# Applying the S5 norm factor at PSUM eviction of the output projection's first half instead of on its input

## The chip, the cores and the metric

The kernel runs on one core of a Trainium2 chip. Its engines work side by side, each from its own queue in program order: TensorE (PE, matmuls; PEld is its weight load), VectorE (DVE), ScalarE (ACT), GpSimd (POOL) and SyncE (SP, which only issues transfers here). The metric is the device time of one execution in microseconds.

## What is computed

One layer of a decoder for 320 token columns (256 of a prompt and 64 of eight short samples): a gated delta-rule group of eight heads and an S5 group, whose outputs are joined into one output projection, then a SwiGLU feed-forward block. What matters here, cut from the reference:

```
y5 = jax.nn.gelu(y5.reshape(bsz, t, MIX_B)).astype(x.dtype)
ab = y5 @ w_glu
y5 = ab[..., :MIX_B] * jax.nn.sigmoid(ab[..., MIX_B:])
y5 = rmsnorm(y5, g_s5_out)

mix = jnp.concatenate([o, y5], axis=-1) @ w_out
```

`rmsnorm` divides each token by the root of its mean square and multiplies by a gain per channel (`g_s5_out`). Tokens are columns here, so the norm is one factor per column, the same for all channels, and the gain is one per row.

## The kernel before

Activations are stored transposed: 128 channels by 320 tokens a tile, 16 tiles for the model's 2,048 channels. To reach nearly full fp32 accuracy with the faster fp32r matmul, both operands are split into a high and a low part (hi, lo), and `mm3` issues three matmuls for each 128x128 weight tile: hi by hi, hi by lo, lo by hi. Such a trio is called a group below; the trace shows it as two `ps_mm<-hT,whi` and one `ps_mm<-hT,wlo`. Weights arrive by DMA as `raw` tiles (512 KB, from SP's queue, line 472), ScalarE makes `whi` (line 501) and VectorE `wlo` (line 502); twelve weight buffers are shared by raw, hi and lo.

The order on every engine is fixed when the program is built. The main sequence is a list of weight segments (`Seg`), and after each group `tick` lets background generators (`bg`) add instructions whose inputs a planner's clock believes ready. An engine then works through its queue in that order and stands where an instruction's inputs are late. Several background generators run in the stretch of this change: the eight heads of the delta rule (`delta`, with `sample` for the sample columns), which use the PSUM tiles `ps_bA` and `ps_bB`; and the modulation (`ada`, `ps_ax`), whose segments are mixed into the list.

The stretch goes so. The GLU of the S5 group (`body_g`, `body_a`) makes eight tiles y5(m), kept in `u`, and squares of them are summed in `sqa` (the last one in `sql`, which has the name `gt` in the trace). Then `y5_norm` multiplies both by a matrix of ones to get the sum over channels in every row, takes Ln and Exp for the factor r, and for each of the eight tiles multiplies by r in place, takes a slot of the tag `h`, and writes hi and lo with the gain into a tile `hT`. The output projection's first half (`first_pair` for output tiles 0 and 1, `first_half` for tiles 2 to 15) contracts these eight tiles: 16 output tiles by 8 groups, 128 groups. `store` copies each result from PSUM (two banks of `ps_mm`) on ScalarE into `u` (tiles 0 to 7) or `M` (8 to 15). The second half contracts the eight heads' outputs (`hz` in the trace) and adds. The heads must all be done by its start.

SP's queue is in order too: a weight load placed behind a store of a head's result is issued only when that store's data exist.

Of the kernel before, what the change touches and what calls it, by code (L numbers as in the profile page):

```python
# [10 lines left out]
F32 = mybir.dt.float32  # L11
F32R = mybir.dt.float32r
AF = mybir.ActivationFunctionType
OP = mybir.AluOpType
# [9 lines left out]
N = NP + NS  # L24
# [86 lines left out]
class Layer:  # L111
# [2015 lines left out]
    def mixer(self):  # L2127
        I = self.I

        self.items += self.ada_set(self.ADA[0], self.ADA[1])  # L2130
        self.yps = {}
        self.y5 = lambda m: self.u[:, m].rearrange("p h w -> p (h w)")[:, :N]
        act_y = lambda kt: (self.yT[kt][:, 0], self.yT[kt][:, 1])
        glu, self.gt5 = [], {}
        for m in range(8):
            def body_g(s, m=m):
                self.await_(lambda: len(self.yT) == 8 and self.npg == 0)
                self.npg += 1
                ps = self.mbank()
                self.mm3(s, ps[:, :N], 0, act_y, True, True)  # L2140
                self.pend += 1
                self.bg(self.glu_gate(m, ps), front=True)

            def body_a(s, m=m):
                self.await_(lambda: self.nga == 0)
                self.nga += 1
                ps = self.mbank()
                self.mm3(s, ps[:, :N], 0, act_y, True, True)
                self.pend += 1
                self.bg(self.glu_tail(m, ps), front=True)  # L2150

            glu.append(Seg(I["w_glu"][0], 0, 8, 1024 + m * 128, 128, body_g))
            glu.append(Seg(I["w_glu"][0], 0, 8, m * 128, 128, body_a))
        self.items += merge(glu, self.ada_set(self.ADA[1], self.ADA[2]))
        self.fn(lambda: self.give("h", 8))
        self.fn(lambda: self.bg(self.y5_norm(), front=True))
        self.items += self.ada_set(self.ADA[2], self.ADA[3])
        wo = I["w_out"][0]
        self.M = [None] * 16
        act_m = lambda kt: (self.mT[kt][:, 0], self.mT[kt][:, 1])  # L2160

        def first_half(s, m):
            self.await_(lambda: all(k in self.mT for k in range(8, 16)))
            ps = self.mbank()
            self.mm3(s, ps[:, :N], 0, act_m, True, True)
            store(m, ps)

        def first_pair(s):
            self.await_(lambda: all(k in self.mT for k in range(s.k0, s.k0 + 4)))
            self.nomm = s.k0 == 8  # L2170
            if self.nomm:
                self.wps = self.mbank(), self.mbank()
            for m in range(2):
                self.mm3(s, self.wps[m][:, :N], m, act_m, s.k0 == 8, s.k0 == 12)
                if s.k0 == 12:
                    store(m, self.wps[m])

        def store(m, ps):
            if m < 8:
                self.M[m] = self.y5(m)  # L2180
            elif m % 2 == 0:
                self.await_(lambda: self.used["h"] < self.CAP["h"])
                self.used["h"] += 1
                t = self.htmp("M")
                self.M[m], self.M[m + 1] = t[:, 0:N], t[:, N:2 * N]
            self.copy(self.M[m], ps[:, :N])

        a = [Seg(wo, k0, 4, 0, 256, first_pair) for k0 in (8, 12)]
        a += [Seg(wo, 8, 8, m * 128, 128, lambda s, m=m: first_half(s, m)) for m in range(2, 16)]
        self.items += merge(a, self.ada_set(self.ADA[3], self.ADA[4]))  # L2190

        def heads():
            self.give("h", 8)

        self.fn(heads)

        def second_half(s, m):
            self.await_(lambda: all(k in self.mT for k in range(8)))
            if m == 0:
                self.post_start(0, 2, "g_post_mix")  # L2200
            ps = self.mbank()
            self.mm3(s, ps[:, :N], 0, act_m, True, True)
            self.pend += 1
            self.bg(self.post_chunk(m, ps, 2), front=True)

        self.items += [Seg(wo, 0, 8, m * 128, 128, lambda s, m=m: second_half(s, m)) for m in range(16)]
# [15 lines left out]
    def glu_tail(self, m, ps):  # L2222
        while m not in self.gt5:
            yield
        t = self.gt5.pop(m)
        y = self.y5(m)
        yield from self.p.stt(y, t[:, :N], 1.0, ps[:, :N], OP.add, OP.mult)
        self.nga -= 1
        self.pend -= 1
        yield  # L2230
        if m == 0:
            yield from self.take("xw")
        yield from self.acc_square(y, m == 0, t, m == 7)
        if m == 7:
            return
        self.give("xw")
# [20 lines left out]
    def y5_norm(self):  # L2257

        while self.nsq < 7:
            yield  # L2260
        r = self.sql
        yield from self.until("PE", (), (self.sqa[:, :N], self.sql[:, :N]))
        while self.bank_free("mm") > self.clk["now"]:
            yield
        ps = self.bank("mm")
        self.mm(ps[:, :N], self.onesc, self.sqa[:, :N], True, False)
        self.mm(ps[:, :N], self.onesc, self.sql[:, :N], False, True)
        self.act(r[:, :N], ps[:, :N], AF.Ln, scale=1.0 / 4096, bias=self.c_eps)
        self.exp(r[:, :N], r[:, :N], scale=-0.5, bias=self.c_lnh)
        yield  # L2270
        g = self.gcols("g_s5_out")
        for m in range(8):
            y = self.y5(m)
            yield from self.p.mul(y, y, r[:, :N])
            yield
            yield from self.take("h")
            hl = self._slot(self.hp.tile([128, 2, N], F32R, name="hT", tag="h", bufs=self.hbufs), "h", self.hbufs)
            yield from self.p.act(hl[:, 0], y, AF.Copy, scale=g[:, m:m + 1])
            yield
            yield from self.p.stt(hl[:, 1], y, g[:, m:m + 1], hl[:, 0].bitcast(F32), OP.mult, OP.subtract)  # L2280
            self.mT[8 + m] = hl
        self.give("xw", 2)


    def post_start(self, i, gate, g):
# [267 lines left out]
def merge(a, b):  # L2553

    out, i, j = [], 0, 0
    while i < len(a) or j < len(b):
        if j * len(a) < i * len(b) and j < len(b) or i >= len(a):
            while b[j].hold:
                out.append(b[j])
                j += 1  # L2560
            out.append(b[j])
            j += 1
        else:
            out.append(a[i])
            i += 1
    return out
# [37 lines left out]
```

## Time and profile before

| | us |
|---|---|
| three runs | 1861.14, 1871.71, 1873.30 (median 1871.71) |
| the profiled execution | 1872.74 |
| its span from first to last instruction | 1871.0 |
| TensorE busy | 1774.1 (95%) |
| VectorE busy | 961.3 (51%) |
| ScalarE busy | 763.8 (41%) |
| GpSimd busy | 316.8 (17%) |
| mean granted TensorE clock | 0.969 of full |

A row of a timeline gives start, length, engine, line, operation, output<-inputs, count, and in brackets how long the engine stood idle before and what released it. Matmul lengths overlap (a weight load and the next matmul begin before one ends), so distances between starts are used for TensorE's pace. [...]

### The profile page before, as it was taken

Reading aid. Unit: us, or ns where it says so; the run is one execution under the profiler, and the core shown is the slowest. Engines: PE = TensorE matmul, PEld = TensorE weight load, DVE = VectorE, ACT = ScalarE, POOL = GpSimd, SP = SyncE. Lnnn points to the kernel's source line nnn. Section 1 sums busy time; section 2 is a strip of 40 time slices with the busy share of each in tenths; the row PEclk is TensorE's granted clock in tenths of the full one; section 3 lists DMA queues with packets and bytes.
Section 4 is the critical chain, followed back from the end, with each engine's and each line's share of the span. In section 5 each row is a group of like instructions: output and inputs, shape, how many; then the busy total and the mean of one; then the engine's idle time right before and its main releaser. Section 6 shows DMA issues by size and latency. Waiting matters only on the chain.

```text
span 1871.0 us, 32687 instructions
## 1 busy us (share of the span) xinstructions
PE 1774.1 (95%) x12971; PEld 1609.3 (86%) x12971; DVE 961.3 (51%) x1798; ACT 763.8 (41%) x1438; POOL 316.8 (17%) x429
## 2 busy tenths in 40 slices
PE   7899998899999898998999999999999999999998
PEld 4778996666787676897799999999999999999997
DVE  3677733888756356444734334344443444444445
ACT  3433334575643255443534333333333333333343
POOL 1000184656031221026500000000000000000043
PEclk9999988999999897999999999999999999999999
DMA  8998644767848762867555566554565545655452
GB/s 277 304 357 282 173 103 141 207 188 212 265 139 268 227 185 84 261 191 236 171 169 169 155 185 178 150 153 120 153 176 150 147 121 153 177 148 153 124 144 86
DMA packets 501262, 340.66 MB, mean 182 GB/s; under 512 B 45355, under 2 KB 452619, under 8 KB 500781
## 3 DMA queue, kind: packets, MB, share of 16 engines
q1 hardware_dynamic: 483904, 332.41, 59.7%
q10 hardware_dynamic: 16838, 5.93, 1.3%
q8 instruction: 102, 1.67, 0.4%
q14 instruction: 50, 0.41, 0.1%
q0 software_dynamic: 368, 0.24, 0.1%
HBM read 323.22 MB, written 14.54 MB: 181 GB/s over the span
## 4 chain that ended last, share of the span: by engine, by line
PE 59%; DVE 2%; ACT 1%; POOL 0%; DMA 0%; issue 0%; SPq 0%; POOLq 0%; DVEq 0%
PE ps_mm L319 30%; PE ps_bA L319 14%; PE ps_bB L319 14%; PE ps_ax L319 1%; DVE acc L281 1%; DVE u L281 1%; DVE wlo L502 0%; ACT whi L501 0%; PE ps_bA L333 0%; POOL h2t L281 0%; DMA S<-in_state_delta_dram 0%; ACT rs L264 0%; PE ps_mm L333 0%; ACT ch L264 0%; ACT yo L264 0%
## 5 line engine op out<-in xcount | busy, mean ns | idle before, releaser
L502 DVE TENSOR_TENSOR wlo<-raw,whi 128x1024 fp32r<-128x1024 f32 (+2 forms) x441 | 502.0, 1141 | 596.7 <-ACT whi L501 376.4
L501 ACT ACTIVATE whi<-raw 128x1024 fp32r<-128x1024 f32 (+2 forms) x441 | 423.9, 965 | 415.7 <-DVE wlo L502 307.3
L319 PE MATMUL ps_mm<-h,whi 128*128 128x320 f32 x1344 | 296.4, 308 | 0.0
L319 PE MATMUL ps_mm<-hT,whi 128*128 128x320 f32 x1204 | 290.4, 328 | 4.6 <-ACT whi L501 1.8
L319 PEld LDWEIGHTS ps_mm<-hT,whi 128*128 128x128 f32 x1204 | 203.9, 195 | 27.7 <-issue 15.7
L319 PEld LDWEIGHTS ps_mm<-h,whi 128*128 128x128 f32 x1344 | 224.5, 187 | 0.8 <-issue 0.8
L319 PE MATMUL ps_mm<-h,wlo 128*128 128x320 f32 x672 | 206.7, 308 | 0.0
L319 PE MATMUL ps_mm<-hT,wlo 128*128 128x320 f32 x602 | 191.5, 318 | 4.0 <-DVE wlo L502 4.0
L319 PE MATMUL ps_bA<-h,whi 128*128 128x320 f32 x736 | 164.6, 311 | 1.9 <-ACT whi L501 1.9
L319 PE MATMUL ps_bB<-h,whi 128*128 128x320 f32 x736 | 162.6, 308 | 0.0
L319 PE MATMUL ps_mm<-f,whi 128*128 128x320 f32 x704 | 155.6, 308 | 0.0
L281 POOL TENSOR_TENSOR sqa<-acc 128x320 f32<-128x320 f32 x1 | 0.7, 722 | 854.0 <-DVE acc L281 854.0
L319 PEld LDWEIGHTS ps_bA<-h,whi 128*128 128x128 f32 x736 | 125.0, 191 | 2.1 <-ACT whi L501 2.1
L319 PEld LDWEIGHTS ps_mm<-h,wlo 128*128 128x128 f32 x672 | 125.9, 187 | 0.0
L319 PEld LDWEIGHTS ps_bB<-h,whi 128*128 128x128 f32 x736 | 122.8, 187 | 1.7 <-issue 1.7
L319 PEld LDWEIGHTS ps_mm<-hT,wlo 128*128 128x128 f32 x602 | 117.0, 194 | 6.5 <-DVE wlo L502 6.3
L319 PEld LDWEIGHTS ps_mm<-f,whi 128*128 128x128 f32 x704 | 117.6, 187 | 0.8 <-ACT whi L501 0.8
L319 PE MATMUL ps_bA<-h,wlo 128*128 128x320 f32 x368 | 114.5, 311 | 0.4 <-DVE wlo L502 0.4
L319 PE MATMUL ps_bB<-h,wlo 128*128 128x320 f32 x368 | 113.2, 308 | 0.0
L319 PE MATMUL ps_mm<-f,wlo 128*128 128x320 f32 x352 | 108.5, 308 | 0.4 <-DVE wlo L502 0.4
L319 PE MATMUL ps_ax<-raw,cs 128*32 128x512 f32 (+2 forms) x832 | 100.3, 591 | 6.0 <-DMA raw<-in_w_ada_dram 6.0
L319 PE MATMUL ps_mm<-hx,whi 128*128 128x320 f32 x328 | 82.4, 337 | 5.0 <-ACT whi L501 4.9
(561 smaller groups left out, 2883.4 us busy)
## 6 DMA issues: line engine op xcount, KB each, us to landing
raw<-in_w_ada_dram SPq DMA_DIRECT2D x180, 512.0 KB
raw<-in_w_gate_dram SPq DMA_DIRECT2D x88, 512.0 KB
raw<-in_w_up_dram SPq DMA_DIRECT2D x88, 512.0 KB
raw<-in_w_in_dram SPq DMA_DIRECT2D x66, 512.0 KB
raw<-in_w_down_dram SPq DMA_DIRECT2D x64, 512.0 KB
raw<-in_w_out_dram SPq DMA_DIRECT2D x32, 512.0 KB
raw<-in_w_down_dram SPq DMA_DIRECT2D x64, 192.0 KB
raw<-in_w_glu_dram SPq DMA_DIRECT2D x16, 512.0 KB
```

What stands on the lines that cost most here:

```text
L281: return e.tensor_tensor(out, a, b, op=op)
L319: return self.T.matmul(out, lhsT, rhs, start=start, stop=stop)
L501: return (self.S.activation(s.hi[:, :w], s.raw[:, :w], AF.Copy), self.V.tensor_tensor(s.lo[:, :w], s.raw[:, :w], s.hi[:, :w].bitcast(F32), ...
L502: self.V.tensor_tensor(s.lo[:, :w], s.raw[:, :w], s.hi[:, :w].bitcast(F32), op=OP.subtract))
```

## The change

r moves from the input of the first half to its output. Since r is one factor per token column and the projection sums over channels, it can be taken out of the sum. `y5_split(m)` makes hi and lo of y5(m) times the gain as soon as y5(m) exists and an `h` slot is free; eight of them are registered as background work, two at a time. `y5_norm` only computes r, into the tile `rsb`, which the first stage no longer needs; its two matmuls of ones go to a bank of `ps_bA` or `ps_bB`, as background work. `store` waits until r has been placed in the program, and instead of a copy on ScalarE multiplies the PSUM result by r on VectorE.

```diff
@@ mixer
+        self.y5r, self.y5_done = None, set()
         self.fn(lambda: self.bg(self.y5_norm(), front=True))
+        self.fn(lambda: self.bg([self.y5_split(m) for m in range(8)], k=2, front=True))
@@ store
-            self.copy(self.M[m], ps[:, :N])
+            self.await_(lambda: self.y5r is not None)
+            self.mul(self.M[m], ps[:, :N], self.y5r)
@@ glu_tail
+        self.y5_done.add(m)
@@ y5_norm
-        r = self.sql
-        yield from self.until("PE", (), (self.sqa[:, :N], self.sql[:, :N]))
-        while self.bank_free("mm") > self.clk["now"]:
-            yield
-        ps = self.bank("mm")
-        self.mm(ps[:, :N], self.onesc, self.sqa[:, :N], True, False)
-        self.mm(ps[:, :N], self.onesc, self.sql[:, :N], False, True)
-        self.act(r[:, :N], ps[:, :N], AF.Ln, scale=1.0 / 4096, bias=self.c_eps)
-        self.exp(r[:, :N], r[:, :N], scale=-0.5, bias=self.c_lnh)
-        yield
-        g = self.gcols("g_s5_out")
-        for m in range(8):
-            y = self.y5(m)
-            yield from self.p.mul(y, y, r[:, :N])
-            yield
-            yield from self.take("h")
...
-            yield from self.p.act(hl[:, 0], y, AF.Copy, scale=g[:, m:m + 1])
-            yield
-            yield from self.p.stt(hl[:, 1], y, g[:, m:m + 1], hl[:, 0].bitcast(F32), OP.mult, OP.subtract)
-            self.mT[8 + m] = hl
+        r = self.rsb
+        ps = yield from self.bget()
+        yield from self.p.mm(ps[:, :N], self.onesc, self.sqa[:, :N], True, False)
+        yield from self.p.mm(ps[:, :N], self.onesc, self.sql[:, :N], False, True)
+        yield
+        yield from self.p.act(r, ps[:, :N], AF.Ln, scale=1.0 / 4096, bias=self.c_eps)
+        yield from self.p.exp(r, r, scale=-0.5, bias=self.c_lnh)
+        self.bput(ps)
         self.give("xw", 2)
+        self.y5r = r
+    def y5_split(self, m):
+        while m not in self.y5_done:
+            yield
+        yield from self.take("h")
...
+        yield from self.p.act(hl[:, 0], y, AF.Copy, scale=g)
+        yield
+        yield from self.p.stt(hl[:, 1], y, g, hl[:, 0].bitcast(F32), OP.mult, OP.subtract)
+        self.mT[8 + m] = hl
```

Because the planner places everything anew, the order changes on all engines from the end of the GLU to the start of the second half; outside this stretch it is the same.

On TensorE, right after the last group of the GLU, the kernel before has this (`sqa,onesc` and `gt,onesc` are the norm's two matmuls; `S,Z`, `sP,kb`, `kr,LAs` belong to a head's samples, `xcat` and `ch` to the heads):

```order
L319 MATMUL ps_bA<-S,Z 32x128 x8
L333 MATMUL ps_bA<-ident,xcat 64x128 x2
L333 MATMUL ps_bA<-ident,kr 128x64
L319 MATMUL ps_mm<-sqa,onesc 128x320
L319 MATMUL ps_mm<-gt,onesc 128x320
L319 MATMUL ps_bA<-sP,kb 128x128 x2
L319 MATMUL ps_bA<-S,Z 32x128 x8
L333 MATMUL ps_bA<-ident,xcat 64x128 x2
L333 MATMUL ps_bA<-ident,ch 128x128 x2
L333 MATMUL ps_bB<-ident,xcat 128x128 x4
L319 MATMUL ps_bA<-kr,LAs 64x128
L319 MATMUL ps_bA<-sP,kb 128x128 x2
```

and the changed kernel, from the third of these rows on:

```order
L333 MATMUL ps_bA<-ident,kr 128x64
L319 MATMUL ps_mm<-hT,whi 128x320 x2
L319 MATMUL ps_mm<-hT,wlo 128x320
...
L319 MATMUL ps_bA<-sP,kb 128x128 x2
L319 MATMUL ps_mm<-hT,whi 128x320 x2
L319 MATMUL ps_mm<-hT,wlo 128x320
L319 MATMUL ps_bA<-sqa,onesc 128x320
L319 MATMUL ps_bA<-gt,onesc 128x320
L319 MATMUL ps_mm<-hT,whi 128x320 x2
L319 MATMUL ps_mm<-hT,wlo 128x320
L319 MATMUL ps_bA<-kr,LAs 64x128
L319 MATMUL ps_bA<-S,Z 32x128 x8
```

The dots stand for two more groups. Before, the first group of the output projection comes 24 rows behind the norm's matmuls; now four stand ahead of them. Ahead of the last matmul of a head (`ident,ch`) stand 55 of the 128 groups, in 34 blocks between heads' rows; in the kernel before it is 34 groups in 22 blocks.

On VectorE, behind the last GLU product (`u<-gt,ps_mm`), the kernel before has the multiplies by r (`u<-u,gt`), each with its lo part (`hT<-u,gv,hT`) spread among the heads' rows:

```order
L306 SCALAR_TENSOR_TENSOR u<-gt,ps_mm 128x320
L306 SCALAR_TENSOR_TENSOR z<-ps_bA,gv,z 128x64
L299 TENSOR_SCALAR kr<-ps_bA,dk 64x128 x2
L306 SCALAR_TENSOR_TENSOR Z<-xcat,sx 128x8x8
L281 TENSOR_TENSOR Z<-xcat,sx 128x8x8
L281 TENSOR_TENSOR u<-u,gt 128x320
```

and the changed kernel:

```order
L306 SCALAR_TENSOR_TENSOR u<-gt,ps_mm 128x320
L306 SCALAR_TENSOR_TENSOR hT<-u,gv,hT 128x320 x4
L306 SCALAR_TENSOR_TENSOR z<-ps_bA,gv,z 128x64
L299 TENSOR_SCALAR kr<-ps_bA,dk 64x128 x2
L306 SCALAR_TENSOR_TENSOR hT<-u,gv,hT 128x320 x2
L281 TENSOR_TENSOR kr<-kr,ps_bA 64x128
```

Four lo parts now stand ahead of the head's `z` and `kr`, which TensorE's `sP,kb` waits for.

On SP, the kernel before has, behind the load of a sample head's states:

```order
L690 DMA out_dram<-ch 128x128 x2
L690 DMA out_dram<-S 128x128
L690 DMA out_dram<-S 128x4x128 x2
L472 DMA raw<-in_w_out_dram 128x8x128
L472 DMA raw<-in_w_ada_dram 128x2x512 x3
L690 DMA S<-in_state_delta_dram 128x4x128 x2
```

and the changed kernel:

```order
L690 DMA out_dram<-ch 128x128 x2
L472 DMA raw<-in_w_out_dram 128x8x128
L472 DMA raw<-in_w_ada_dram 128x2x512 x3
L690 DMA out_dram<-S 128x128
L472 DMA raw<-in_w_ada_dram 128x2x512
L690 DMA out_dram<-S 128x4x128 x2
L690 DMA S<-in_state_delta_dram 128x4x128 x2
```

One load of `w_out` and four of `w_ada` stand ahead of stores they followed before.

## Rows read from the trace of the kernel before

**Rows 1.** The page: busy times; slices' clock; the chain that ended last, by engine.

```profile
PE 1774.1 (95%) x12971; PEld 1609.3 (86%) x12971; DVE 961.3 (51%) x1798; ACT 763.8 (41%) x1438; POOL 316.8 (17%) x429
PEclk9999988999999897999999999999999999999999
PE 59%; DVE 2%; ACT 1%; POOL 0%; DMA 0%; issue 0%; SPq 0%; POOLq 0%; DVEq 0%
```

**Rows 2.** Table by stretch, TensorE alone, GLU's end to second half's start.

```profile
697.15:707.25 10.10, 6.47 (x61) 0.99 0.43 125
707.25:730.66 23.41, 22.59 (x77) 0.50 0.23 69
730.66:741.60 10.94, 6.95 (x46) 0.97 0.49 146
741.60:744.48 2.88, 2.84 (x24) 0.50 0.73 219
744.48:768.19 23.71, 23.71 (x159) 1.00 0.45 127
768.19:817.54 49.35, 46.61 (x321) 1.00 0.96 295
```

**Rows 3.** Timeline, TensorE: a norm row, waits for heads, the first group.

```profile
699.72 0.70 PE L319 MATMUL ps_mm<-gt,onesc 128*128 128x320 f32 x2
700.95 0.68 PE L319 MATMUL ps_bA<-sP,kb 128*128 128x128 f32 x4 [0.53 <-DVE kr L299]
738.17 0.62 PE L333 MATMUL ps_bA<-ident,ch 128*128 128x128 f32 x2 [1.84 <-ACT ch L264]
717.31 0.88 PE L319 MATMUL ps_mm<-hT,whi 128*128 128x320 f32 x2
```

**Rows 4.** By tile `u`, 697 to 818 us: count, min/median/max ns, first and last start.

```profile
L281 DVE TENSOR_TENSOR u<-u,gt x8: 477/484/898, 701.6 to 740.0; 128x320 f32<-128x320 f32 x8
L264 ACT ACTIVATE hT<-u,gv x8: 545/561/563, 703.4 to 740.6; 128x320 fp32r<-128x320 f32 x8
L306 DVE SCALAR_TENSOR_TENSOR hT<-u,gv,hT x8: 533/545/603, 706.1 to 742.0; 128x320 fp32r<-128x320 f32 x8
L264 ACT ACTIVATE u<-ps_mm x8: 417/430/440, 749.1 to 783.1; 128x320 f32<-128x320 f32 x8
```

**Rows 5.** Groups by shape: VectorE 817-874 us, ScalarE 748-818, TensorE 697.15-817.54.

```profile
L281 DVE TENSOR_TENSOR u<-ps_mm,u 128x320 f32<-128x320 f32 x8 | 3.9, 482 | 0.0
L264 ACT ACTIVATE M<-ps_mm 128x320 f32<-128x320 f32 x8 | 3.5, 438 | 20.4 <-PE ps_mm L319 20.4
L319 PE MATMUL ps_ax<-raw,cs 128*32 128x512 f32 x64 | 7.7, 598 | 0.0
```

**Rows 6.** Timeline, TensorE: groups next to each other, behind and ahead of heads' rows.

```profile
757.34 0.46 PE L319 MATMUL ps_mm<-hT,whi 128*128 128x320 f32 x2
757.78 0.45 PE L319 MATMUL ps_mm<-hT,whi 128*128 128x320 f32 x2
758.22 0.38 PE L319 MATMUL ps_bA<-ch,L 128*128 128x128 f32 x2
758.36 0.54 PE L319 MATMUL ps_mm<-hT,whi 128*128 128x320 f32 x2
765.25 0.38 PE L333 MATMUL ps_bA<-ident,ch 128*128 128x128 f32 x2
```

**Rows 7.** Table by stretch, TensorE alone, the GLU among the heads' work.

```profile
540.00:560.00 20.00, 20.00 (x165) 1.00 0.28 86
560.00:580.00 20.00, 19.19 (x142) 1.00 0.72 205
617.00:641.00 24.00, 19.91 (x249) 0.95 0.98 276
641.00:657.00 16.00, 13.83 (x346) 0.54 0.19 68
```

**Rows 8.** SP's own timeline; x is the number of transfers issued.

```profile
699.57 22.47 SPq L690 DMA_DIRECT2D out_dram<-S  x3
```

More of the change, by code (lines that the diff above doesn't have):

```diff
@@ L2260, in y5_norm @@
             yield
-        r = self.sql
-        yield from self.until("PE", (), (self.sqa[:, :N], self.sql[:, :N]))
-        while self.bank_free("mm") > self.clk["now"]:
-            yield
-        ps = self.bank("mm")
-        self.mm(ps[:, :N], self.onesc, self.sqa[:, :N], True, False)
-        self.mm(ps[:, :N], self.onesc, self.sql[:, :N], False, True)
-        self.act(r[:, :N], ps[:, :N], AF.Ln, scale=1.0 / 4096, bias=self.c_eps)
-        self.exp(r[:, :N], r[:, :N], scale=-0.5, bias=self.c_lnh)
-        yield
-        g = self.gcols("g_s5_out")
-        for m in range(8):
-            y = self.y5(m)
-            yield from self.p.mul(y, y, r[:, :N])
-            yield
-            yield from self.take("h")
-            hl = self._slot(self.hp.tile([128, 2, N], F32R, name="hT", tag="h", bufs=self.hbufs), "h", self.hbufs)
-            yield from self.p.act(hl[:, 0], y, AF.Copy, scale=g[:, m:m + 1])
-            yield
-            yield from self.p.stt(hl[:, 1], y, g[:, m:m + 1], hl[:, 0].bitcast(F32), OP.mult, OP.subtract)
-            self.mT[8 + m] = hl
-        self.give("xw", 2)
+        r = self.rsb
[6 more added lines that the diff above has]
+        self.bput(ps)
+        self.give("xw", 2)
+        self.y5r = r
+    def y5_split(self, m):
+        while m not in self.y5_done:
+            yield
+        yield from self.take("h")
+        g = self.gcols("g_s5_out")[:, m:m + 1]
+        y = self.y5(m)
+        hl = self._slot(self.hp.tile([128, 2, N], F32R, name="hT", tag="h", bufs=self.hbufs), "h", self.hbufs)
+        yield from self.p.act(hl[:, 0], y, AF.Copy, scale=g)
+        yield
+        yield from self.p.stt(hl[:, 1], y, g, hl[:, 0].bitcast(F32), OP.mult, OP.subtract)
+        self.mT[8 + m] = hl
     def post_start(self, i, gate, g):
```

## The prediction, made before the changed kernel ran

> **What bounds the kernel now.** I read the page first, then the table by stretch around the change, then the timeline of TensorE inside the stretches that are not full, and last the rows of the operations that are moved. The page says that TensorE is busy 95% of the span, far ahead of the others, and that the chain that ended last is 59% TensorE with little else [rows 1]. Time can be gained, then, only where TensorE stands still or runs at the low clock. The slices' clock shows few such places [rows 1]; the lowest, the 7 of slice 16 (702 to 748 us), lies in the stretch of the change: from the GLU's last group (697.15 us) to the first matmul of the second half (817.54), 120.39 us.
>
> The table by stretch takes it apart [rows 2]. From 697.15 to 707.25 TensorE is busy 6.47 of 10.10 us: 3.63 idle. Then its clock falls to 0.50 for 23.41 us, in which it is busy 22.59. From 730.66 to 741.60 it is back near full but idle for 3.99 us, then at 0.50 again for 2.88. From 744.48 on it is full, and from 768.19 to 817.54 it is idle 2.74 us of 49.35.
>
> Why it stands is in the timeline [rows 3]. After the norm's two matmuls (the last at 699.72) TensorE has nothing but heads' work, and each head is a chain through ScalarE and VectorE: `sP,kb` waits 0.53 us for VectorE, `ident,ch` 1.84 us for ScalarE. The first group of the output projection starts at 717.31. Between stand r's Ln and Exp, and then eight times multiply, hi, lo, spread among the heads' rows: the multiplies start from 701.6 to 740.0 and the last lo part at 742.0 [rows 4]. The projection's 128 groups are the work that could cover the heads, and they come too late for it.
>
> **The change part by part.**
>
> *What could be gained.* Idle time before 744.48: 3.63 + 0.82 + 3.99 + 0.04 = 8.48 us. Low clock: the busy time there took twice as long as at 1.00, so half of it is lost: (22.59 + 2.84) / 2 = 12.72. Together 21.2 us. The 2.74 us idle from 768.19 on [rows 2] lie behind the heads, where the order hardly changes and the DMA engines are 0.96 busy; I leave them.
>
> *What now feeds TensorE.* The order puts three groups right behind the GLU's last products and 55 among the heads' rows. They need hi and lo of y5 only. The first tiles' hi parts need nothing of the last GLU group; on VectorE four lo parts follow the last GLU product, 4 x 0.545 = 2.2 us [rows 4], and TensorE takes a group each 0.44 us [rows 6], so it follows them closely. Behind these four stand the head's `z` and `kr`, for which `sP,kb` waits [rows 3]; that wait may grow by about 2.2 us less the 1.3 us of three groups, some 0.9.
>
> *What idle time stays.* Without the idle time and at full clock TensorE has 120.39 - 11.22 - 12.72 = 96.45 us of work here. Behind the last head's matmul stand 73 groups (32.1 us) and two of the four modulation sets (7.7 / 2 = 3.9 us [rows 5]), so the mixed part is some 60 us. How full TensorE is when groups and heads are mixed is seen in the GLU [rows 7]: idle 0 and 0.81 us of 20 in two stretches, and 4.09 of 24 in the worst at nearly full clock. I take 6%, between the first two (0 to 4%) and the last (17%): 3.6 us, with 0 and 10 us as the ends. It takes the growth of the wait in.
>
> *Finer mixing.* There are 12 more changes from heads to groups. A group's first rows last 0.54 behind a head's row against 0.45 behind a group [rows 6], so at most 12 x 0.09 = 1.1 us, at least nothing since rows overlap; I take 0.5.
>
> *The multiplies.* Eight from SBUF fall away on VectorE (0.484 us median [rows 4]), and 16 copies on ScalarE, 8 x 0.430 and 8 x 0.438 [rows 4, 5], 6.9 us. In their place stand 16 multiplies of a PSUM tile by an SBUF tile on VectorE. The trace of before has no such multiply; the nearest row is the addition in the same form, `u<-ps_mm,u`, 482 ns [rows 5], and the slowest neighbour is 898 [rows 4], the ends 0.43 (a copy) and 0.90. I take 0.48: 7.7 us on VectorE, 3.8 more than before. VectorE's whole load is 51% [rows 1], and a ps_mm bank is needed again only after another output tile, 8 groups or 3.5 us, so at 0.48 or at 0.90 it costs nothing. Were that cover gone, each of 16 tiles would add at most 0.48 - 0.43 = 0.05 us, under 1 us in all. [...]
>
> *The norm's factor.* Its two matmuls, Ln and Exp stay. The wait for r moves from the first group to the first `store`, twelve groups later (12 x 0.44 = 5.3 us of TensorE alone, more with heads between). r needs two matmuls and two ScalarE operations of about half a microsecond. If it is late, TensorE can work on in the second ps_mm bank for four more groups. What is late next is the heads' own chain.
>
> *The queues.* SP stood 22.47 us at three stores of heads' states [rows 8], with a load of w_out and three of w_ada behind. The order now puts these loads and a fourth of w_ada ahead of most of the stores. I give it no gain.
>
> *Sum.* 21.2 - 3.6 - 0.5 = 17.1 us. The profiled execution took 1872.74 us (span 1871.0), 1.0 above the median of the three runs, 1871.71. 1872.7 - 17.1 gives 1855.6, say **1856 us**. About 1%, or 19 us, is what a measurement of this kernel can tell from no change: the three runs themselves lie 12 us apart.
>
> **The rivals.**
>
> *The clock falls all the same.* With heads' short waits between groups TensorE may still drop to 0.50. For it: from 641 to 657 it ran at 0.54 although groups were mixed in [rows 7]. Against it: that followed a stretch idle for 17%, with many small matmuls; the other mixed stretches ran at 1.00. If a period as long as the one of before (22.59 us busy) came back, 11.3 us of the gain would go: 17.1 - 11.3 = 5.8, 1867 us. [...]
>
> *The change doesn't do what it says.* TensorE works in order, so a group cannot pass a head's matmul that waits. If each head's wait stays and the groups only stand between, the idle time and the clock stay as they are: 0 to 3 us gained, 1871 us. Against it: a head's chain runs on ScalarE and VectorE while groups run, and where groups were dense, 744.48 to 768.19, TensorE lost nothing [rows 2].
>
> *Slower: the weights wait for the heads.* SP's loads of w_out stand between stores of heads' states. If the 34 blocks of groups hold up the heads' chains, the stores come later, and the loads behind them too. Five segments of w_out (40 groups, 17.6 us) are ahead of the first of these stores, and the heads' own work on TensorE is about 34 us (60 less 55 groups and a modulation set); it decides once SP stands there longer than both together, some 50 us, against 22.47 before [rows 8]. If each of the 40 groups held up the chain, the heads would end 17.6 us later than the 765.25 of before [rows 6], at 783; if the 49.35 us behind them [rows 2] stay, since the loads can't run ahead, the second half begins at 832, 15 us later than 817.54: 1887 us.
>
> *All of it and more.* If the mixed part were as full as 744.48 to 768.19, and the loads that are issued earlier also closed the 2.74 us, 21.2 + 2.7 = 23.9 us would go: 1849 us.
>
> **How the numbers follow.** Forecast (12 to 21 us gained) 0.62; the clock falls 0.15; nothing gained 0.10; all and more 0.07; slower 0.06. The range leaves out the last 0.06 and the 0.10 with nothing gained, and a little at the low end: 1846 to 1869. It holds the clock rival and the end of the idle share at 10 us (1862). Faster by over 1% means under 1853: all of "all and more" and, of the forecast, the part with over 18.7 us gained, about 0.25 of the 0.62: 0.32. Slower 0.06. The rest, 0.62, is within 1%.
>
> **What would show it.** In the profile after: the first `ps_mm<-hT` within 3 us of 697 rather than at 717; the clock at 1.00 from 700 to 800; from the GLU's end to the first `hz` about 103 us, not 120; TensorE idle 3 to 4 us in the mixed part; `u<-ps_mm,rsb` near 480 ns with no TensorE wait released by it. I am wrong if the clock row still shows 0.50 for more than a few us, if the waits on `kr` and `ch` keep their sizes, or if TensorE waits for `whi` from late w_out loads.

## The result: 1 % faster, a little more than forecast

| | before | changed |
|---|---|---|
| median of four runs each, us | 1866.43 (1858.24 to 1873.30) | 1846.32 (1843.53 to 1850.07) |
| span of the profiled execution, us | 1871.0 | 1846.5 |
| from the GLU's last group to the second half, us | 120.39 | 98.60 |

The ratio is 0.9889, with a 95% interval of 0.9858 to 0.9921: between 0.8 and 1.4% faster. A second comparison (under "The two kernels once more") gave 0.9871 (0.9834 to 0.9909). The forecast was 1856 us and "within 1%"; the time lies at the lower edge of the range.

The page of the changed kernel, TensorE's busy time and the clock of the 40 slices:

```profile
PE 1756.6 (95%) x12971; PEld 1597.3 (87%) x12971; DVE 963.8 (52%) x1806; ACT 757.9 (41%) x1422; POOL 316.6 (17%) x429
PEclk9899999999999999998999999999999999999999
```

TensorE issues as many instructions as before and is busy 17.5 us less [rows 1]: more of them ran at the full clock (its mean over the span is 0.981 of full, against 0.969). The 7 of slice 16 is gone. The table by stretch of the stage (start and end, length, TensorE busy and its instructions, granted clock with 1.00 as full, DMA share, GB/s) answers to [rows 2], which has the same columns:

```profile
695.10:705.20 10.10, 9.14 (x83) 1.00 0.77 227
705.20:730.00 24.80, 24.41 (x172) 1.00 0.51 150
730.00:752.00 22.00, 21.51 (x145) 1.00 0.59 159
752.00:793.70 41.70, 41.30 (x287) 1.00 1.06 316
```

The four lengths sum to 98.60 us, the busy times to 96.36. TensorE stands still for 2.23 us in all, and the clock never leaves 1.00. So 21.79 us of the 24.5 us between the two spans are won here: 11.22 - 2.23 = 8.99 us of idle time, and the 12.72 of low clock (the 0.08 us left over is busy time).

TensorE's timeline shows what fills the place where [rows 3] had only heads' work:

```profile
695.92 0.64 PE L319 MATMUL ps_bA<-S,Z 128*32 128x128 f32 x16 [0.82 <-DVE Z L281]
697.03 0.55 PE L319 MATMUL ps_mm<-hT,whi 128*128 128x320 f32 x2
698.75 0.68 PE L319 MATMUL ps_bA<-sP,kb 128*128 128x128 f32 x4
700.26 0.70 PE L319 MATMUL ps_bA<-gt,onesc 128*128 128x320 f32 x2
```

The first group starts 1.93 us after the GLU's end instead of 20.16 us, three groups stand ahead of `sP,kb`, and `sP,kb` waits for nothing. The norm's two fp32 matmuls of 128x320, `sqa,onesc` at 699.72 and `gt,onesc` at 700.26, start 0.54 us apart; the three fp32r matmuls of a group, of the same size, take 0.44 us together [rows 6]. Of all waits of TensorE in the stage, the list (total, times, longest) has only two rows:

```profile
PE ps_mm L319 <- DVE wlo L502: 1.3, 3, 0.5
PE ps_bA L319 <- DVE Z L281: 0.8, 1, 0.8
```

The tile `rsb`, which holds r, shows the new eviction and the factor itself (count, shortest/median/longest ns, first and last start):

```profile
L281 DVE TENSOR_TENSOR u<-ps_mm,rsb x8: 469/482/492, 712.1 to 760.6; 128x320 f32<-128x320 f32 x8
L281 DVE TENSOR_TENSOR M<-ps_mm,rsb x8: 485/492/494, 764.0 to 793.9; 128x320 f32<-128x320 f32 x8
L264 ACT ACTIVATE rsb<-rsb,cc x1: 562/562/562, 705.4 to 705.4; 128x320 f32<-128x320 f32 x1
```

r exists at 706.0 us; the first product that needs it starts at 712.1, 6 us later.

### The profile page after: what moved, and what is told of

It is laid out like the page before. It is cut to its first block, busy times and chain, and to the rows that moved or that the text cites. A ratio compares the mean times of both kernels' runs of the same rounds, so it can differ in the third digit from the quotient of the medians.

```text
span 1846.5 us, 32677 instructions
## 1 busy us (share of the span) xinstructions
PE 1756.6 (95%) x12971; PEld 1597.3 (87%) x12971; DVE 963.8 (52%) x1806; ACT 757.9 (41%) x1422; POOL 316.6 (17%) x429
## 4 chain that ended last, share of the span: by engine, by line
PE 76%; DVE 7%; DMA 5%; POOL 4%; ACT 4%; issue 2%; SPq 1%; ACTq 0%; POOLq 0%; DVEq 0%
PE ps_mm L319 37%; PE ps_bA L319 20%; PE ps_bB L319 14%; PE ps_ax L319 2%; DMA raw<-in_w_in_dram 2%; POOL bx L281 2%; DVE wlo L502 2%; POOL AB L281 1%; ACT whi L501 1%; DVE ca L306 1%; DMA hist<-in_state_conv_dram 1%; DMA ts<-ts 1%; SPq L472 1%; PE ps_bB L333 1%; DVE acc L281 1%
```

## The experiments

All are read by one stage, from the GLU's last group to the first matmul of the second half. TensorE's useful work in it is 96.4 us at full clock, in the kernel before as worked out in the prediction and in the changed one as measured. Idle time is read from the table by stretch (length less busy time); what is left of the stage is what the low clock cost. Each ratio is to the kernel before as it ran beside that kernel.

| kernel | stage | idle | lost to the low clock | time, median | ratio to before |
|---|---|---|---|---|---|
| before, three profiles | 120.39, 120.09, 117.54 | 11.2, 10.8, 12.0 | 12.7, 12.9, 9.2 | | |
| changed, two profiles | 98.60, 98.49 | 2.2, 2.1 | 0, 0 | 1846.32, 1841.48 | 0.9889, 0.9871 |
| late split | 113.20 | 10.4 | 6.4 | 1858.30 | 0.9948 |
| norm in the background, two profiles | 109.00, 108.67 | 6.8, 6.5 | 5.8, 5.8 | 1854.26 | 0.9931 |
| copy without the factor | 100.90 | 4.2 | 0.3 | 1850.71 | 0.9921 |
| wait for all eight | 114.70 | 8.2 | 10.1 | 1862.38 | 0.9978 |
| the same with filler | 109.10 | 4.1 | 0 (8.6 of filler) | 1855.92 | 0.9943 |
| groups after r | 110.50 | 11.0 | 3.1 | 1860.50 | 0.9958 |

### The early split taken back

```diff
-        while m not in self.y5_done:
+        while m not in self.y5_done or self.y5r is None:
             yield
```

> The changed kernel, but the hi and lo parts of y5 wait until the factor r has been placed (y5_split waits for y5r too); r is still applied at the eviction. Stage means the time from the end of the GLU's last group to the first hz matmul: 120.4 us before, 98.6 after. Theory (the projection's groups come early enough to cover the heads' waits and to hold TensorE's clock up): without the early start most of the gain goes; the first group comes at least 8 us behind the GLU's end, part of the stretch is at clock 0.50, stage 108 to 119 us, time 1855 to 1868. Rival (the gain is the work that fell out of the chain: eight multiplies by r in place): stage 98 to 103 us, time near 1846.

Time 1858.30 us, ratio 0.9948 (0.9924 to 0.9972): about half of the gain is gone; time and stage lie in the theory's ranges. The table by stretch:

```profile
689.60:700.00 10.40, 7.25 (x66) 1.00 0.77 227
700.00:713.40 13.40, 11.91 (x42) 0.62 0.01 2
713.40:762.00 48.60, 48.23 (x338) 1.00 0.65 194
762.00:802.80 40.80, 35.44 (x241) 1.00 0.90 268
```

The stage is 14.6 us longer than in the changed kernel. The first group starts 8.10 us after the GLU's end. Two groups further on, TensorE waits once more, for a low part of y5:

```profile
701.49 0.64 PE L319 MATMUL ps_mm<-hT,whi 128*128 128x320 f32 x1 [2.50 <-DVE hT L306]
```

From 689.6 to 701.5 TensorE is idle for 4.65 us in all; then the clock falls for a while. Up to 762 us idle time and low clock cost 9.6 us more than in the changed kernel, and this is the part that the prediction speaks of. The other 5.0 us were not expected: 5.36 us of idle time in the last stretch (0.40 us in the changed kernel's), where the wait list from 762 us on has

```profile
PE ps_mm L319 <- DVE wlo L502: 5.0, 4, 1.5
```

TensorE waits for the low part of late weights. VectorE's rows and TensorE's next to each other show what holds it up:

```profile
774.25 0.49 DVE L281 TENSOR_TENSOR M<-ps_mm,rsb 128x320 f32<-128x320 f32 x1 [3.60 <-PE ps_mm L319]
774.65 1.22 DVE L502 TENSOR_TENSOR wlo<-raw,whi 128x1024 fp32r<-128x1024 f32 x1
775.92 0.41 PE L319 MATMUL ps_mm<-hT,wlo 128*128 128x320 f32 x1 [1.43 <-DVE wlo L502]
```

In VectorE's queue the new multiply of one output tile stands ahead of the `wlo` that the next output tile needs. VectorE stands 3.60 us until TensorE has ended the first tile, multiplies, and only then makes `wlo`, for which TensorE stands 1.43 us. It goes the same way at the next two tiles. So the multiply at eviction is not free in every order. In the changed kernel none of the three waits for `wlo` has such a multiply right ahead of it. Whether a copy on ScalarE would do better in this order was not tried.

### Only the norm moved to the background

This is the kernel before, where y5 is still multiplied by r ahead of the split; only the norm's matmuls, Ln and Exp are placed as the changed kernel places them.

```diff
-        while self.bank_free("mm") > self.clk["now"]:
-            yield
...
-        ps = self.bank("mm")
-        self.mm(ps[:, :N], self.onesc, self.sqa[:, :N], True, False)
+        r = self.rsb
+        ps = yield from self.bget()
+        yield from self.p.mm(ps[:, :N], self.onesc, self.sqa[:, :N], True, False)
...
-            yield from self.p.mul(y, y, r[:, :N])
+            yield from self.p.mul(y, y, r)
```

> The kernel before, with only the norm's two matmuls, Ln and Exp made as in the change (background work, bank of ps_bA or ps_bB, r in rsb); y5 is still multiplied by r ahead of hi and lo. Theory: no gain to speak of, since the first group still waits for r and eight multiplies: stage 114 to 121 us, clock 0.50 in it, time 1860 to 1872. Rival (the main sequence, and with it the heads, was held up by the norm's wait for a ps_mm bank): stage 99 to 106 us, time 1846 to 1853.

> The kernel before with only the norm's two matmuls, Ln and Exp moved into the background, once more. Theory A (the low clock's length belongs to the kernel): 9 to 10 us of low clock and a stage of 109 us within 1 us, as in the run before. Theory B (its length differs between executions): idle time 6.8 us within 1 us as in the run before, low clock anywhere from 0 to 27 us, and a stage longer or shorter by half of the difference.

Time 1854.26 us, ratio 0.9931 (0.9906 to 0.9956); stages of 109.00 and 108.67 us. The expectation of the first run was 114 to 121 us, so it missed. By stretch:

```profile
693.60:704.10 10.50, 6.54 (x63) 0.99 0.44 126
704.10:713.80 9.70, 9.33 (x35) 0.50 0.09 27
713.80:768.00 54.20, 52.50 (x356) 1.00 0.68 218
768.00:802.60 34.60, 33.83 (x234) 1.00 0.99 270
```

The first 10 us are those of the kernel before: the same idle time (3.96 us against 3.63 [rows 2]), the first group 20.05 us after the GLU's end, the clock falling. What is better lies behind: 1.70 us idle from 713.80 to 768 where before there were 3.99 us in one stretch alone, 0.77 us at the end, and a shorter low clock. Both profiles agree in this. So small an edit, which the prediction costed at nothing, is worth half of the gain or more: 11.4 of 21.8 us of the stage. With the early split as well the stage falls by another 10.4 us; what the split alone would bring, without the norm's new place, no run here shows. The gain lies in the heads' work: the last matmul of a head comes 57.1 us after the GLU's end,

```profile
750.68 0.42 PE L333 MATMUL ps_bA<-ident,ch 128*128 128x128 f32 x2
```

against 68.1 us before (765.25 [rows 6]), and what follows it takes as long as before. Why the heads end sooner was not settled. The rival, that the norm's wait for a `ps_mm` bank held them up, stays open; its stage of 99 to 106 us was missed too. SP's order doesn't explain it, since SP stands at the stores nearly as long as before [rows 8]:

```profile
696.31 20.84 SPq L690 DMA_DIRECT2D out_dram<-S  x3
```

### The copy on ScalarE put back, without the factor

```diff
-            self.mul(self.M[m], ps[:, :N], self.y5r)
+            self.copy(self.M[m], ps[:, :N])
```

> The changed kernel with the first half's results copied out of PSUM by ScalarE as before, without the factor r (left out of the computation). Theory (the multiply on VectorE is hidden): stage 97.5 to 99.5 us as in the changed kernel, time within 0.3% of it. Rival (VectorE is the next limit in the stretch, its multiplies delay the wlo splits and the heads): stage 93 to 97 us, and the three waits of TensorE for wlo (1.3 us) shrink.

Time 1850.71 us, ratio 0.9921 (0.9893 to 0.9950), and a stage of 100.90 us at a clock of 1.00:

```profile
697.30:798.20 100.90, 96.66 (x682) 1.00 0.76 225
```

```profile
L264 ACT ACTIVATE u<-ps_mm 128x320 f32<-128x320 f32 x8 | 3.4, 431 | 3.3 <-PE ps_mm L319 3.1
```

The copies are back at 431 ns on ScalarE, and nothing is gained: the stage is 2.3 us longer than the changed kernel's, 1.4 us outside what the theory had, and the waits for `wlo` are no shorter (1.9 us against 1.3). In the changed kernel's order the sixteen multiplies on VectorE are hidden; where the eviction runs is not what the change is worth.

### TensorE kept at work, and its control

Both kernels are the kernel before with the first group waiting for all eight tiles. The one called filler puts matmuls of ones by the identity, which nobody reads, wherever TensorE's program would otherwise be empty in that wait.

```diff
+                if self.fill is None:
                     self.clk["now"] += 0.2
+                else:
+                    self.mm(self.fill[:, :128], self.onesc, self.ident, True, True)
...
-            self.await_(lambda: all(k in self.mT for k in range(s.k0, s.k0 + 4)))
+            if s.k0 == 8:
+                self.fill = self.bank("ax")
+                self.await_(lambda: all(k in self.mT for k in range(8, 16)))
+                self.fill = None
```

> The kernel before, where first_pair waits at once for all eight hT tiles, and wherever the order would leave TensorE with nothing in that wait a 128x128 fp32 matmul of ones by the identity goes to the unused ps_ax bank (some 40 of them, 0.22 us each); its result is read by nobody. No group covers a head's wait here, but TensorE is kept at work. Theory of the clock (of the 21.8 us that the stage lost, 12.7 are the low clock, and the clock falls because TensorE stands still after the GLU): the clock stays at 1.00, or low for under 10 us; against e5, which is the same without the filler, the stage is 6 to 13 us shorter. Rival (the clock falls with heads' small matmuls, busy or not): the clock still falls for about 20 us, and the stage is as long as e5's or longer by the filler's 8 us.

> The kernel before, where first_pair waits at once for all eight hT tiles; no filler. The control for e4. Theory: the ten groups that stood among the heads before 742 us go behind, so the stage is longer than before: 120 to 130 us, low clock for 20 us or more, time 1866 to 1880. Rival (the early groups cover nothing since TensorE works in order): stage 118 to 121.

The control took 1862.38 us (0.9978; 0.9954 to 1.0002), the filler 1855.92 (0.9943; 0.9922 to 0.9964). The control's stage of 114.70 us missed both its expectation (120 to 130) and the rival's (118 to 121): it begins as the kernel before does,

```profile
698.90:709.50 10.60, 6.58 (x62) 0.98 0.43 123
709.50:727.00 17.50, 17.14 (x60) 0.53 0.22 62
727.00:733.00 6.00, 4.05 (x34) 0.99 0.19 55
733.00:736.00 3.00, 2.86 (x12) 0.50 0.38 109
```

and loses 10.1 us to the clock; but behind the first stretch it is idle for only 4.2 us, where the kernel before is for 7.6 [rows 2]. Taking the early groups out of that stretch did not cost what the expectation had put on it. The filler's table, and the row of the useless matmuls (count, busy us, mean ns; the lengths overlap):

```profile
693.90:726.00 32.10, 30.01 (x238) 1.00 0.34 96
726.00:768.00 42.00, 41.37 (x285) 1.00 0.76 246
768.00:803.00 35.00, 33.64 (x232) 1.00 0.96 267
```

```profile
L320 PE MATMUL ps_ax<-ident,onesc 128*128 128x128 f32 x68 | 10.4, 281 | 0.0
```

With the useless work the clock stays at 1.00 over the whole stage. TensorE does 105.02 us of work there, 8.6 more than is needed, and the stage is still 5.6 us shorter than the control's, just under the 6 to 13 expected. The two programs differ in more than the filler: the planner's clock moves on with each useless matmul, so later rows come in another order (the first group 28.3 us after the GLU's end against 35.5). But up to the control's `ident,ch` at 708.00 us, just ahead of the fall of its clock, the order on TensorE is the same but for the filler. When its clock fell the control had been idle for 4.0 of 10.6 us; the filler's kernel was idle for 2.1 of its first 10.8 us and then no more up to 726. So in these two kernels the clock falls where TensorE stands still and holds where most of the holes are filled, with 10.1 us lost against none.

### The early split kept, the groups held until r

```diff
             self.await_(lambda: all(k in self.mT for k in range(s.k0, s.k0 + 4)))
+            self.await_(lambda: self.y5r is not None)
```

> The changed kernel with the early hi and lo parts, but the output projection's first group waits until r has been placed; in the order four matmul rows of heads and the norm's stand ahead of the first group that stood behind it. Theory (the groups' start is what counts): the first group comes some 5 to 8 us later than in the changed kernel, TensorE is idle for 3 to 5 us before it, the clock stays up or falls for under 10 us: stage 101 to 110 us, time 1848 to 1858. Rival (what counts is that hi and lo are out of the heads' way on VectorE and ScalarE): stage 98 to 100, time as the changed kernel.

Time 1860.50 us, ratio 0.9958 (0.9937 to 0.9979); stage 110.50 us: stage and time lie just above the theory's ranges (101 to 110, 1848 to 1858) and far above the rival's.

```profile
700.60:712.00 11.40, 9.01 (x83) 1.00 0.70 207
712.00:768.00 56.00, 54.58 (x379) 1.00 0.60 184
768.00:800.00 32.00, 24.81 (x151) 0.89 0.79 236
```

Here the first group comes 8.3 us after the GLU's end, about as late as in the kernel with the late split, and yet the clock holds there: no second wait follows, and TensorE is idle for 2.39 us in the first stretch, against 4.65 in that kernel. The loss is at the end, 7.19 us idle from 768 to 800 us and a fall of the clock in it. The wait list of that stretch has two rows:

```profile
PE ps_mm L319 <- DVE wlo L502: 5.2, 4, 1.4
PE ps_mm L319 <- DVE u L281: 2.0, 1, 2.0
```

ScalarE's rows and one of VectorE's:

```profile
772.29 0.33 ACTq L690 DMA_DIRECT2D xr<-xTd  x1
772.66 1.19 ACT L264 ACTIVATE hz<-z 128x320 fp32r<-128x320 f32 x3 [9.12 <-DMA raw<-in_w_out_dram]
782.58 0.49 DVE L281 TENSOR_TENSOR M<-ps_mm,rsb 128x320 f32<-128x320 f32 x1 [6.20 <-PE ps_mm L319]
```

ScalarE stands for 9.12 us ahead of `hz`; the trace puts it down to a weight load, and ScalarE issues a load of its own (`xr`) directly before. VectorE, in order, then makes the low parts of `hz` late and, behind them, the multiply that frees a `ps_mm` bank: the 2.0 us. From there on it goes as with the late split: VectorE stands at a multiply at eviction (6.20 us here, then three times 3.6), with the `wlo` of the next tile behind it, and TensorE waits for `wlo`. ScalarE's stand at this place is 7.02 us in the kernel with the late split and 0.82 in the changed kernel; that it brings the late waits about was not tested. The wait for r in this place costs 12 us, but most of it not where r is waited for.

### The two kernels once more

> The changed kernel itself, for comparison on the same chip as e4 to e6, and to see how far its stage moves from one execution to the next: 98 to 101 us, clock 1.00 in it, ratio 0.985 to 0.992. Were the gain a chance of one execution's clock, the stage would be over 105 us.

```profile
688.43:786.92 98.49, 96.36 (x683) 1.00 0.79 230
```

> The kernel before once more, unchanged, to see whether the length of the low clock belongs to the kernel or to the execution. Theory A (it belongs to the kernel): about 26 us of low clock between the GLU's last group and the second half's first matmul, as in the first profile, and a stage of 118 to 123 us. Theory B (how much idle time TensorE has sets only that the clock falls; how long it stays low differs between executions): the same idle time, 11 us within 1 us, but a low clock whose length differs by more than 5 us, and a stage of 108 to 123 us that differs by half of it.

> The kernel before a third time, for the same question. Theory A: a low clock of about 26 us and a stage of 118 to 123 us. Theory B: the same idle time, 11 us, another length of the low clock, and a stage of 108 to 123 us.

The changed kernel's stage repeats within 0.1 us. That of the kernel before doesn't: the second profile is like the first,

```profile
689.11:809.20 120.09, 109.26 (x682) 0.89 0.64 190
```

and the third is not:

```profile
696.43:712.30 15.87, 10.49 (x87) 1.00 0.28 82
712.30:722.55 10.25, 10.25 (x34) 0.51 0.37 97
722.55:732.85 10.30, 8.26 (x56) 0.99 0.34 109
732.85:743.10 10.25, 8.12 (x45) 0.51 0.59 168
```

With the same program and 5.38 us of idle time in the first 15.87, the clock fell 5.8 us later than in [rows 2] and for 10.25 us, and once more for 10.25 us. So in all three profiles the clock falls behind idle time of TensorE; when, and how long it stays low, differs between executions. In the three profiles of one program it cost 12.7, 12.9 and 9.2 us.

## Why the prediction was right on the clock and short on the idle time

**The steps that failed.** Two terms of the sum. The idle time that it leaves in the stage, 3.6 us in the mixed part and 2.74 behind the heads, was too large: 2.23 us were left in all. And the norm's new place has no price in it, though by itself it shortened the stage by 8.5 to 11.7 us. The last step from the sum to "within 1%" failed with them: it took 19 us for what a measurement can tell from no change, and the interval of the result is 6 us to either side.

**Where the time is.** Right. 21.79 of the 24.5 us between the two profiled spans are in the stage that the first paragraphs name. The remaining 2.7 us lie where the order is the same; there the clock differs from one execution to the next (0.93, 0.97 and 0.96 from 250 to 690 us in three profiles of the kernel before).

**The low clock, 12.72 us.** Right, and the largest term: it went to none, in both profiles of the changed kernel. That the idle time brings it about was argued in the prediction; the filler and its control bear it out, with none lost against 10.1 us.

**The idle time of the mixed part, 3.6 us.** Too large. Up to 752 us, which takes in nearly all heads' work (the last `ident,ch` is at 756.13), TensorE stands still for 0.96 + 0.39 + 0.49 = 1.84 us. That is 3% of 56.9 us, in the range of the GLU's two better stretches [rows 7]; its worst, which had drawn the estimate up to 6%, has no counterpart here. The feared growth of the wait on `sP,kb` behind four lo parts did not come: three groups of TensorE's own were in front of it.

**The 2.74 us behind the heads, left in.** Wrong. It is 0.40 us after 752. Together with the 0.5 us for finer mixing, which is not to be seen (96.36 us of work against 96.45), these three terms are 1.8 + 2.3 + 0.6 = 4.7 us, just the difference between the 17.1 us forecast and the stage's 21.8. Two sentences of the prediction belong to it: that the order behind the heads hardly changes, and that SP's new order gains nothing. SP's longest stand at a store in the stage fell from 22.47 us [rows 8] to

```profile
727.18 4.20 SPq L690 DMA_DIRECT2D out_dram<-S  x3
```

and the loads behind run ahead. But that this closed the gap is not shown: with the norm in the background alone SP stood for 20.84 us and TensorE still waited only 0.77 us at the end, and with the late split no store held SP for as long as 3 us, and TensorE waited for 5.36. Where the late wait came, in the late split and in the groups after r, VectorE stood at a multiply at eviction with the next tile's `wlo` behind it; so by the traces the order of these two on VectorE sets it there, though no run with the two exchanged was made.

**The norm's factor.** Right that r is not late (6 us to spare). Wrong that its place gains nothing: placed alone, it gave between 8.5 and 11.7 us of the stage, by the three profiles of before and the two of that kernel. The prediction asked what the step would delay and not what it had held up. In the sum this hides behind the other terms, since the idle time and the low clock that it takes away are counted there as the early groups' gain. That the total came so near is in part luck.

**The multiplies at eviction.** Right for the changed kernel: 482 and 492 ns against 480 forecast, no wait of TensorE released by them, and no gain from the copy. Too general, though: the prediction looked at the `ps_mm` bank alone and not at what stands behind the multiply on VectorE, which cost over 4 us (three waits of 1.4 us) in each of two experiments. The multiply of a PSUM tile by one in SBUF took 482 and 492 ns in the median here, that of two tiles in SBUF 484 in the kernel before [rows 4].

**The rivals.** The clock did not fall: it was 1.00 from 695.10 to 793.70 us, with the two `ps_mm` banks cycled among heads' matmuls up to the last `ident,ch` at 756.13. The "weights wait for the heads" rival did not come here, but its kind, a late weight, did in two of the experiments, at 5.0 and 5.2 us: it was the right thing to fear, from another cause than SP's stores. "All of it and more", 23.9 us at a chance of 0.07, is the nearest to what the stage shows, and was given too little.

**The level and the chances.** The time was 9.7 us under the forecast. By the medians the gain is 20.1 us, 3.0 more than the 17.1 forecast, and its interval, 14.7 to 26.5 us, holds both. The larger part is the base: the sum was made from 1872.7 us, one of the longer executions of the kernel before, whose four runs have a median of 1866.4, 6.3 us less. "Within 1%" was chosen because 17.1 us is 0.9%; with 19 us as the border, two microseconds decided the class, and 0.62 against 0.32 was more than the working could carry.

## What to carry to other kernels

Where TensorE is the bound, ask first what it could do while a norm is formed: a factor per column can wait until the product leaves PSUM. Its multiply there was hidden in the changed kernel, with 1.3 us of waits for `wlo`; in the late split and in the groups after r, where VectorE stood at such a multiply with the next tile's `wlo` behind it, these waits were 5.0 and 5.2 us. The 12.7 us lost to the low clock were won back whole here when the holes ahead of it were filled, but the loss in one profile is one draw of several: 12.7, 12.9 and 9.2 us in three of the kernel before. When an order is planned anew, look at the last wait of the stage as well as the first: small edits moved the idle time there between 0.4 and 7.2 us.

## What was not expected of the chip

With TensorE at work all the time (10.25 us busy of 10.25), the granted clock stayed at 0.51 through that stretch in the third profile of the kernel before, and at 0.50 for 23.41 us with 22.59 busy in the first [rows 2]: in these stretches work alone did not bring it back at once, and not after the same time. Over the stage one program lost between 9.2 and 12.9 us to it. And useless matmuls paid: 8.6 us of them made the stage 5.6 us shorter.
